# Three-pass float32 products in a gated linear attention block: normalized rows stored split instead of split again in each sweep

## The chip, the cores and the metric

The kernel runs on one core of one Trainium2 chip. The metric is the device time of one execution in microseconds; where several executions are given, the median counts.

## The reference, cut to what matters

One layer of a chunked encoder on 2048 tokens of width 1024. The part that the change touches:

```
h = rmsnorm(x, mix_norm_w)
q, k, v, r, glr = split(h @ gla_w_in)
g = cumsum(log_sigmoid(glr @ w_gate2 + b_gate) / 16)     # in chunks of 64
for each chunk:
    state = state * exp(g_end) + (k * exp(g_end - g)).T @ v
    o = (q / sqrt(128)) @ state
x = x + (rms_normalize(o) * norm_w * silu(r)) @ gla_w_out
x = x + conv_ffn(rmsnorm(x, ffn_norm_w))
out = rmsnorm(x, final_norm_w)
```

## The kernel before, in words

TensorE's float32r operand holds fewer bits than a float32. So every operand is **split** into two float32r tiles: `hi`, a rounded copy made on ScalarE (a CAST), and `lo`, the difference, made on VectorE; the helper `split` (L183 to L186) issues both. A product is then three matmuls (`mm3p`, L173): hi by lo, lo by hi, hi by hi.

The matrix products are cut in seven, after Strassen and Winograd: two token tiles of 128 (a pair `j`, 8 pairs in all) and two column halves make a two by two block matrix, whose seven sums of blocks are called p1 to p7 and run in the order p1, p5, p6, p7, p4, p2, p3. A **row** below is one such sum of normalized input blocks: 128 partitions by 512 float32, 256 KB. There are 56 of them.

The attention part is four sweeps over the 8 pairs, each with other weights (`PS = "RABY"`):

- R makes the rows from x (normalize, transpose, sums), splits each, multiplies it for the gates and for r, and stores the float32 row in DRAM (`h1d`, L368).
- A and B load the 56 rows again, split each again, and multiply for k, q and v of two heads each. Beside the products the scan runs: `scan_tile` (L621) with its small matmuls `pk` and `po`, its transposes `pq` and `px`, and the states `sh`, `sl`. So A and B are the scanning sweeps. `scan_loads` (L604) fetches r from DRAM, and a Silu on ScalarE stands right behind it (L609).
- Y loads scan outputs (`yd`), splits them too and multiplies by w_out.

After that come the two halves of the feed-forward part: U (w_up, with the convolution) and D (w_down). The last 1324 us belong to these.

`prep_row` (L428) fetches a row. In A, B and Y a raw tile (`row_tile`, tag `hr`, `HB = 4` buffers of 2 KB a partition) is loaded for the row itself and the two after it, then `split_row` writes a pair tile (`w_pair`, tag `w`, `WB = 4` buffers of 4 KB). `limit` (L860) says how many rows are prepared before a product: two ahead (`LEAD = 2`). All row loads and stores go through SP's queue, with the loads of r and of E, and the stores of scan outputs. The weights of the next sweep are prepared in the one before: `make_sums` (L264), at pairs 2 and 4, loads weight blocks through ScalarE's queue, adds them on VectorE and stores the sums (`wsd`) through SP's; `plan_w` (L333) then splits the weights around the seam of two sweeps.

The order of instructions on each engine is made ahead of time by a list scheduler that follows the program's priorities and a model of durations; on the chip each engine works through its list in order, DMA issues included.

```
t = w_pair(f"h_{ps_}{j}_{o}")                       # L365
split(t[:, 0, :], t[:, 1, :], src)
if ps_ == "R":
    nc.sync.dma_start(h1d[j, o], src)
```

Of the kernel before, what the change touches and what calls it, by code (L numbers as in the profile page):

```python
# [10 lines left out]
F32 = mybir.dt.float32  # L11
F32R = mybir.dt.float32r
# [4 lines left out]
P = 128  # L17
# [3 lines left out]
def f32(ap):  # L21
    return ap.bitcast(F32)
# [3 lines left out]
def hybrid_kernel(  # L26
# [36 lines left out]
    WB = 4  # L63
    WX = 3
    AB = 6
    HB = 4
    RB = 4
    SB = 8
    YB = 7
    LEAD = 2  # L70
    DLY, KLY, XLY = 5.0, 2.0, 6.5
    NLY, NLE = 5.5, 9.0
    Y0, Y1, U0, U1 = 3.0, 2.8, 14.0, 11.0
# [37 lines left out]
    def scratch(shape, name):  # L111
        return dr.tile(shape, F32, tag=name, name=name)

    x1d = [scratch([P, D], f"x1d_{t}") for t in range(NTT)]
    h1d = {(j, o): scratch([P, 512], f"h1d_{j}_{o}") for j in range(NP) for o in PORD}
    ed = [scratch([P, H * DK], f"ed_{t}") for t in range(NTT)]
    rd = [[scratch([P, 512], f"rd_{t}_{g}") for g in range(2)] for t in range(NTT)]
    yd = {(j, o): scratch([P, 512], f"yd_{j}_{o}") for j in range(NP) for o in PORD}
# [15 lines left out]
    def w_pair(name):  # L134

        return wp.tile([P, 2, 512], F32R, tag="w", name=name, bufs=WB)
# [227 lines left out]
    def split_row(ps_, j, o, src):  # L364
        t = w_pair(f"h_{ps_}{j}_{o}")  # L365
        split(t[:, 0, :], t[:, 1, :], src)
        if ps_ == "R":
            nc.sync.dma_start(h1d[j, o], src)  # L368
        rows[ps_, j, o] = t[:, 0, :], t[:, 1, :]


# [50 lines left out]

    hraw = {}

    def row_tile(name):
        return wp.tile([P, 512], F32, tag="hr", name=name, bufs=HB)

    def prep_row(ps_, j, o):  # L428
        if ps_ == "R":
            need(f"h{j}")  # L430
            if o == "p4":
                diff(j, o, *hsrc.pop(("p4", j)))
            split_row(ps_, j, o, hsrc.pop((j, o)))
        else:
            m = jobs.index((ps_, j, o))
            for n in range(m, min(m + HB - 1, len(jobs))):
                if jobs[n] not in hraw:
                    p_, j_, o_ = jobs[n]
                    hraw[jobs[n]] = row_tile(f"hr_{p_}{j_}_{o_}")
                    nc.sync.dma_start(hraw[jobs[n]], (yd if p_ == "Y" else h1d)[j_, o_])  # L440
            split_row(ps_, j, o, hraw.pop((ps_, j, o)))


# [326 lines left out]
    def prep_h2(jj, raw, pair):  # L770

        s, j = divmod(jj, PAIRS)
        ts = {}
        held = []

        def load(n, c, k):
            if s == 0:
                ts[n] = h2.pop((2 * jj + c, k))
                return
            if n not in ts:  # L780
                ts[n] = raw(f"h2r_{jj}_{n}")
            nc.sync.dma_start(ts[n], h2f[2 * jj + c][:, k, :])

        def store():
            while held:
                o, hl = held.pop(0)
                if s == 0:
                    nc.sync.dma_start(hd[s, o, j], f32(hl))
                else:
                    for i in range(2):  # L790
                        nc.scalar.dma_start(hd[s, o, j][:, i, :], f32(hl[i]))

        def step(o, n, x=None, y=None, then=None):
            store()
            if x is not None:
                nc.vector.tensor_sub(ts[n], ts[x], ts[y])
            if then is not None:
                then()
            hl = pair(f"h2p_{jj}_{o}")
            hi, lo = hl if s else (hl[:, 0, :], hl[:, 1, :])  # L800
            split(hi, lo, ts[n])
            held.append((o, hl))
            later_do(HLY[s], store)

        def first():
            for n, (c, k) in enumerate(((0, 0), (1, 0), (1, 1))):
                load(n, c, k)

        def last():
            store()  # L810
            ready.add(f"h2p{jj}")

        return [
            first, lambda: step("p1", 0), lambda: step("p5", 0, 1, 0), lambda: step("p7", 1, 2, 1),
            lambda: step("p3", 2, then=lambda: load(1, 0, 1)), lambda: step("p6", 0, 2, 0),
            lambda: step("p2", 1), lambda: step("p4", 1, 1, 0), last,
        ]
# [42 lines left out]
    def limit(ps_, j, i):  # L860

        own = (PS.index(ps_) * NP + j + 1) * len(PORD)
        n = own - len(PORD) + i + 1 + LEAD
        if ps_ == "R" and j == 0 and i < len(PORD) - 2:
            return min(n, i + 2)
        if ps_ == "R" and j + 1 < NP:
            return min(n, own + max(0, i - 4))
        return n
# [146 lines left out]
    def phase_u():  # L1015
# [96 lines left out]
        for k, (s, g, o, f) in enumerate(jobs):  # L1112
# [7 lines left out]
            if k == 6:  # L1120
                while delayed:
                    heapq.heappop(delayed)[-1]()
                yp["ctx"].close()
                pools["ctx"] = ExitStack()
                pools["us"] = pools["ctx"].enter_context(tc.tile_pool(name="us", bufs=1, reuse_waits="tile"))
                pools["wx"] = pools["ctx"].enter_context(tc.tile_pool(name="wx", bufs=1, reuse_waits="tile"))
                spread(range(PAIRS, 2 * PAIRS), U0, U1, row_tile,
                       lambda name: tuple(pools["us"].tile([P, 512], F32R, tag="as", name=f"{name}_{i}", bufs=AB) for i in range(2)))
            if s == NS - 1 and g == NQ - 1 and f % 2 == 0:
                d_early(o)  # L1130
# [272 lines left out]
```

## Time and profile before

| what | value |
|---|---|
| median of 3 executions | 2235.53 us (2234.98 to 2243.4) |
| the profiled execution | 2241.04 us |
| its span | 2238.9 us |
| TensorE busy | 2126.9 us (95%) |
| TensorE weight loads busy | 1741.8 us (78%) |
| VectorE busy | 1642.1 us (73%) |
| ScalarE busy | 1107.5 us (49%) |
| moved by DMA | 411.78 MB, mean 184 GB/s |
| mean granted TensorE clock | 0.985 |

Busy times are unions of an engine's instruction intervals; matmuls overlap each other in the records, so the mean length of one (about 0.39 us) is longer than the step from one to the next. The granted clock is a share of full speed (2.4 GHz; the other level is 1.2 GHz). Idle time on an engine that nobody waits for costs nothing.

### The profile page before, as it was taken

The page shows a single profiled execution, that of the slowest core. Times are in us where ns is not written, and L with a number is a line of the kernel's source. Part 1 is how long each engine was busy: PE and PEld are TensorE (multiplying, and loading weights), DVE is VectorE, ACT ScalarE, POOL GpSimd, SP SyncE. Part 2 cuts the span into 40 slices and gives each one's busy share as a digit, 9 for nine tenths or more (in the row PEclk, how much of TensorE's full clock was granted, in tenths as well). Part 3 has the DMA queues.
Part 4 walks back from the last instruction along what each step waited for, and adds up shares of the span by engine and source line. Part 5 has one row for each costly group of instructions (what it writes and reads, how often), then busy time and mean ns, then how long its engine had stood idle before and what let it go on. Part 6 is the DMA issues. An engine that isn't in the chain of part 4 may idle for free.

```text
span 2238.9 us, 29122 instructions
## 1 busy us (share of the span) xinstructions
PE 2126.9 (95%) x9948; PEld 1741.8 (78%) x9948; DVE 1642.1 (73%) x2175; ACT 1107.5 (49%) x2020; POOL 729.1 (33%) x602
## 2 busy tenths in 40 slices
PE   5999999989999899899999999999999999999998
PEld 3788787877887787677787778788888888888886
DVE  7755777788778765388999787797877777557564
ACT  4554655565555576445445444444444543333342
POOL 1000111112111000265566565466655535046100
PEclk9999999999999999999999999999999999999999
DMA  6545684369546799943535428624242468454443
GB/s 209 195 156 185 206 294 126 123 198 325 169 160 196 266 318 335 364 137 123 189 127 163 147 90 282 192 76 136 71 141 71 136 230 321 137 183 151 141 171 116
DMA packets 305077, 411.78 MB, mean 184 GB/s; under 512 B 23694, under 2 KB 160062, under 8 KB 304928
## 3 DMA queue, kind: packets, MB, share of 16 engines
q1 hardware_dynamic: 266156, 346.72, 46.6%
q10 hardware_dynamic: 38772, 63.20, 8.4%
q8 instruction: 78, 1.28, 0.2%
q14 instruction: 71, 0.58, 0.1%
HBM read 266.70 MB, written 143.13 MB: 183 GB/s over the span
## 4 chain that ended last, share of the span: by engine, by line
PE 62%; DVE 14%; DMA 9%; issue 5%; ACT 5%; POOL 3%; SPq 1%; ACTq 0%; DVEq 0%; POOLq 0%
PE pd_p L179 5%; PE pd_p L180 5%; PE pd_p L178 5%; PE ua L178 5%; PE ua L179 5%; PE ua L180 5%; DVE t L1078 4%; PE mp_R L178 2%; PE uc L178 2%; PE uc L180 2%; PE uc L179 2%; PE mp_R L179 2%; PE mp_R L180 2%; DVE uw_p L186 2%; PE mp_A L178 1%
## 5 line engine op out<-in xcount | busy, mean ns | idle before, releaser
L178 PE MATMUL ua<-h_p,uw_p 128*128 128x512 f32 x704 | 280.4, 398 | 24.3 <-ACT c L1060 24.3
L179 PE MATMUL ua<-h_p,uw_p 128*128 128x512 f32 x704 | 278.9, 396 | 0.0
L180 PE MATMUL ua<-h_p,uw_p 128*128 128x512 f32 x704 | 278.5, 396 | 0.0
L1078 DVE SCALAR_TENSOR_TENSOR t<-u,cw,t 128x1024 f32<-128x1024 f32 x176 | 264.2, 1505 | 8.6 <-ACT t L1076 7.5
L179 PE MATMUL pd_p<-dw_p,da 128*128 128x512 f32 x616 | 240.1, 390 | 1.1 <-DVE da L186 1.1
L180 PE MATMUL pd_p<-dw_p,da 128*128 128x512 f32 x616 | 239.9, 389 | 0.0
L178 PE MATMUL pd_p<-dw_p,da 128*128 128x512 f32 x616 | 239.9, 389 | 0.0
L186 DVE TENSOR_TENSOR uw_p<-ur,uw_p 128x512 fp32r<-128x512 f32 x176 | 168.4, 973 | 59.4 <-ACT uw_p L185 52.3
L186 DVE TENSOR_TENSOR da<-da_p,da 128x512 fp32r<-128x512 f32 x154 | 135.6, 933 | 100.5 <-ACT da L185 99.4
L185 ACT CAST da<-da_p 128x512 fp32r<-128x512 f32 x154 | 85.2, 619 | 203.8 <-PE pd_p L180 149.9
L178 PEld LDWEIGHTS ua<-h_p,uw_p 128*128 128x128 f32 x704 | 134.3, 191 | 58.1 <-ACT c L1060 28.6
L185 ACT CAST uw_p<-us 128x512 fp32r<-128x512 f32 x132 | 82.1, 622 | 164.5 <-POOL us L1040 114.1
L186 DVE TENSOR_TENSOR uw_p<-us,uw_p 128x512 fp32r<-128x512 f32 x132 | 122.4, 936 | 53.4 <-ACT uw_p L185 53.0
L180 PEld LDWEIGHTS ua<-h_p,uw_p 128*128 128x128 f32 x704 | 134.2, 191 | 29.9
L179 PEld LDWEIGHTS ua<-h_p,uw_p 128*128 128x128 f32 x704 | 134.4, 191 | 29.4
L178 PE MATMUL uc<-h_p,uw_p 128*128 128x512 f32 x352 | 138.4, 393 | 0.7 <-DMA h_p<-hd_p 0.7
L179 PE MATMUL uc<-h_p,uw_p 128*128 128x512 f32 x352 | 138.1, 392 | 0.0
L180 PE MATMUL uc<-h_p,uw_p 128*128 128x512 f32 x352 | 138.1, 392 | 0.0
L179 PEld LDWEIGHTS pd_p<-dw_p,da 128*128 128x128 f32 x616 | 115.7, 188 | 25.9 <-DVE da L186 1.9
L1076 ACT ACTIVATE t<-u,cw 128x1024 f32<-128x1024 f32 x88 | 109.7, 1247 | 50.9 <-DVE u L1169 43.0
L178 PEld LDWEIGHTS pd_p<-dw_p,da 128*128 128x128 f32 x616 | 115.7, 188 | 24.2
L180 PEld LDWEIGHTS pd_p<-dw_p,da 128*128 128x128 f32 x616 | 115.7, 188 | 23.7
(251 smaller groups left out, 5477.8 us busy)
## 6 DMA issues: line engine op xcount, KB each, us to landing
ur<-in_ffn_w_up_dram SPq DMA_DIRECT2D x168, 256.0 KB, 3.7
da_p<-ad_p SPq DMA_DIRECT2D x154, 256.0 KB, 3.8
h_p<-hd_p SPq DMA_DIRECT2D x56, 512.0 KB, 7.6
ad_p<-as_p SPq DMA_DIRECT2D x88, 256.0 KB, 2.5
ad_p<-t SPq DMA_DIRECT2D x66, 256.0 KB, 3.2
x<-in_x_dram SPq DMA_DIRECT2D x32, 512.0 KB, 4.9
ch<-in_ffn_w_down_dram SPq DMA_DIRECT2D x61, 256.0 KB, 4.0
hr_A_p<-h1d_p SPq DMA_DIRECT2D x56, 256.0 KB, 2.7
```

The lines of the kernel that those rows point to most:

```text
L178: nc.tensor.matmul(ps_ap, ah, bl, start=(first and i == 0), stop=False, **kw)
L179: nc.tensor.matmul(ps_ap, al, bh, start=False, stop=False, **kw)
L180: nc.tensor.matmul(ps_ap, ah, bh, start=False, stop=(last and i == len(pairs) - 1), **kw)
L185: nc.scalar.copy(hi, src)
L186: nc.vector.tensor_sub(lo, src, f32(hi))
L1076: nc.scalar.activation(t, u[:, 2:2 + TS], AF.Identity, scale=cw[:, 2, c:c + 1], bias=cw[:, 3, c:c + 1])
L1078: nc.vector.scalar_tensor_tensor(t, u[:, k:k + TS], cw[:, k, c:c + 1], t, op0=ALU.mult, op1=ALU.add)
```

## The change

Sweep R stores each row as the split pair, hi and lo, 512 KB in place of 256 KB; the store reads the pair tile and so stands behind the split. Sweeps A and B load that pair, straight into a tile that the matmuls read: the 112 CASTs and 112 subtractions of rows in A and B are gone. The `hr` buffers become two of 4 KB a partition in place of four of 2 KB, and A and B use them as pair tiles beside the four `w` tiles, six in all; the loads in A and B are asked for four rows ahead (`ALEAD = 4`), with exceptions in the last pair of B. Sweep Y still splits; there, and where the second half of the feed-forward input is prepared (`prep_h2`), two raw rows share one pair tile.

```diff
--- before.py
+++ after.py
@@ -63,11 +63,11 @@
     WB = 4
     WX = 3
     AB = 6
-    HB = 4
+    HB = 2
     RB = 4
     SB = 8
     YB = 7
-    LEAD = 2
+    LEAD, ALEAD = 2, 4
     DLY, KLY, XLY = 5.0, 2.0, 6.5
     NLY, NLE = 5.5, 9.0
     Y0, Y1, U0, U1 = 3.0, 2.8, 14.0, 11.0
@@ -112,7 +112,7 @@
         return dr.tile(shape, F32, tag=name, name=name)
 
     x1d = [scratch([P, D], f"x1d_{t}") for t in range(NTT)]
-    h1d = {(j, o): scratch([P, 512], f"h1d_{j}_{o}") for j in range(NP) for o in PORD}
+    h1d = {(j, o): scratch([P, 2, 512], f"h1d_{j}_{o}") for j in range(NP) for o in PORD}
     ed = [scratch([P, H * DK], f"ed_{t}") for t in range(NTT)]
     rd = [[scratch([P, 512], f"rd_{t}_{g}") for g in range(2)] for t in range(NTT)]
     yd = {(j, o): scratch([P, 512], f"yd_{j}_{o}") for j in range(NP) for o in PORD}
@@ -365,7 +365,7 @@
         t = w_pair(f"h_{ps_}{j}_{o}")
         split(t[:, 0, :], t[:, 1, :], src)
         if ps_ == "R":
-            nc.sync.dma_start(h1d[j, o], src)
+            nc.sync.dma_start(h1d[j, o], f32(t))
         rows[ps_, j, o] = t[:, 0, :], t[:, 1, :]
 
 
@@ -422,22 +422,29 @@
 
     hraw = {}
 
-    def row_tile(name):
-        return wp.tile([P, 512], F32, tag="hr", name=name, bufs=HB)
+    def row_pair(name, dt=F32):
+        return wp.tile([P, 2, 512], dt, tag="hr", name=name, bufs=HB)
 
     def prep_row(ps_, j, o):
+        m = jobs.index((ps_, j, o))
         if ps_ == "R":
             need(f"h{j}")
             if o == "p4":
                 diff(j, o, *hsrc.pop(("p4", j)))
             split_row(ps_, j, o, hsrc.pop((j, o)))
+        elif ps_ in "AB":
+            n = m - jobs.index(("A", 0, PORD[0]))
+            t = w_pair(f"h_{ps_}{j}_{o}") if n % (WB + HB) < WB else row_pair(f"h_{ps_}{j}_{o}", F32R)
+            nc.sync.dma_start(f32(t), h1d[j, o])
+            rows[ps_, j, o] = t[:, 0, :], t[:, 1, :]
         else:
-            m = jobs.index((ps_, j, o))
-            for n in range(m, min(m + HB - 1, len(jobs))):
+            for n in range(m, min(m + 3, len(jobs))):
                 if jobs[n] not in hraw:
                     p_, j_, o_ = jobs[n]
-                    hraw[jobs[n]] = row_tile(f"hr_{p_}{j_}_{o_}")
-                    nc.sync.dma_start(hraw[jobs[n]], (yd if p_ == "Y" else h1d)[j_, o_])
+                    if (len(jobs) - n) % 2 == 0:
+                        hraw["tile"] = row_pair(f"hr_{p_}{j_}_{o_}")
+                    hraw[jobs[n]] = hraw["tile"][:, (len(jobs) - n) % 2, :]
+                    nc.sync.dma_start(hraw[jobs[n]], yd[j_, o_])
             split_row(ps_, j, o, hraw.pop((ps_, j, o)))
 
 
@@ -778,7 +785,9 @@
                 ts[n] = h2.pop((2 * jj + c, k))
                 return
             if n not in ts:
-                ts[n] = raw(f"h2r_{jj}_{n}")
+                if n != 1:
+                    ts["tile"] = raw(f"h2r_{jj}_{n}")
+                ts[n] = ts["tile"][:, n % 2, :]
             nc.sync.dma_start(ts[n], h2f[2 * jj + c][:, k, :])
 
         def store():
@@ -860,7 +869,9 @@
     def limit(ps_, j, i):
 
         own = (PS.index(ps_) * NP + j + 1) * len(PORD)
-        n = own - len(PORD) + i + 1 + LEAD
+        n = own - len(PORD) + i + 1 + (LEAD if ps_ in "RY" else ALEAD)
+        if ps_ in "AB":
+            return min(n, own) if ps_ == "B" and j + 1 == NP and i < len(PORD) - LEAD else min(n, own + LEAD) if ps_ == "B" and j + 1 == NP else n
         if ps_ == "R" and j == 0 and i < len(PORD) - 2:
             return min(n, i + 2)
         if ps_ == "R" and j + 1 < NP:
@@ -1124,7 +1135,7 @@
                 pools["ctx"] = ExitStack()
                 pools["us"] = pools["ctx"].enter_context(tc.tile_pool(name="us", bufs=1, reuse_waits="tile"))
                 pools["wx"] = pools["ctx"].enter_context(tc.tile_pool(name="wx", bufs=1, reuse_waits="tile"))
-                spread(range(PAIRS, 2 * PAIRS), U0, U1, row_tile,
+                spread(range(PAIRS, 2 * PAIRS), U0, U1, row_pair,
                        lambda name: tuple(pools["us"].tile([P, 512], F32R, tag="as", name=f"{name}_{i}", bufs=AB) for i in range(2)))
             if s == NS - 1 and g == NQ - 1 and f % 2 == 0:
                 d_early(o)
```

The order of the work moves at these places. ScalarE at the first products of sweep A, before (`cp_A` copies a product out of PSUM, `w_A_p` is a weight split, `e` belongs to the gates, `h_A_p` is a row's CAST):

```order
L513 CAST gstk<-pg_2612 32x256
L241 DMA wr_A_2862<-in_gla_w_in_dram 128x2x256
L958 COPY cp_A_2848<-mp_A_2828 128x512
L241 DMA wr_A_2862<-in_gla_w_in_dram 128x2x256
L530 ACT_TABLE_LOAD
L530 ACTIVATE e_0_2870<-pz_0_2868 128x512
L530 ACTIVATE e_1_2874<-pz_1_2872 128x512
L185 CAST w_A_p_2882<-wr_A_2832 128x1024
L958 COPY cp_A_2885<-mp_A_2855 128x512
L185 CAST h_A_p_2889<-hr_A_p_2823 128x512
```

and now:

```order
L520 CAST gstk<-pg_2612 32x256
L241 DMA wr_A_2850<-in_gla_w_in_dram 128x2x256
L185 CAST w_A_p_2870<-wr_A_2823 128x1024
L969 COPY cp_A_2839<-mp_A_2819 128x512
L185 CAST w_A_p_2870<-wr_A_2825 128x1024
L537 ACT_TABLE_LOAD
L537 ACTIVATE e_0_2858<-pz_0_2856 128x512
L537 ACTIVATE e_1_2862<-pz_1_2860 128x512
L969 COPY cp_A_2873<-mp_A_2843 128x512
```

The row's CAST is gone, and a weight CAST stands ahead of the first copy (`wr_A`'s loads are issued by ScalarE itself, `gstk` belongs to the gates). The line numbers of the changed kernel are 5 to 11 higher here. SP's queue in an undisturbed pair of A, before (`hr_A` row loads, `E` and `r` the loads for the scan, `yd` and `b` stores of scan outputs):

```order
L606 DMA E_8_4230<-ed_158 128x256
L440 DMA hr_A_p_4158<-h1d_p_129 128x512
L606 DMA E_9_4263<-ed_159 128x256
L440 DMA hr_A_p_4240<-h1d_p_130 128x512
L440 DMA hr_A_p_4269<-h1d_p_131 128x512
L440 DMA hr_A_p_4331<-h1d_p_132 128x512
L608 DMA r_8_4232<-rd_0_182 128x512
L440 DMA hr_A_p_4363<-h1d_p_133 128x512
```

and now, between the same load of E and the same row:

```order
L613 DMA E_8_4128<-ed_158 128x256
L613 DMA E_9_4158<-ed_159 128x256
L438 DMA h_A_p_4041<-h1d_p_128 128x1024
L438 DMA h_A_p_4059<-h1d_p_129 128x1024
L438 DMA h_A_p_4138<-h1d_p_130 128x1024
L615 DMA r_8_4130<-rd_0_182 128x512
L438 DMA h_A_p_4164<-h1d_p_131 128x1024
L438 DMA h_A_p_4223<-h1d_p_132 128x1024
L715 DMA yd_p_219<-ot_6_4175 128x512
L438 DMA h_A_p_4252<-h1d_p_133 128x1024
```

The second load of E stands ahead of the row loads now, and the load of r two rows earlier among them; the row loads are of twice the size. ScalarE in the second `make_sums` of sweep B, before (`L241` loads of weight blocks into `wm_Y`; `sh` the state's CAST, `og` the squares of the scan's output):

```order
L678 ACTIVATE og_0_5741,ssq_0_5742<-po_0_5728 128x256 x2
L185 CAST sh_1_0_5763<-state_5588 128x512
L241 DMA wm_Y_01_6556<-in_gla_w_out_dram 128x2x512
L185 CAST h_B_p_5827<-hr_B_p_5720 128x512
L707 COPY ot_0_5839<-px_0_5834 128x512
L185 CAST sh_1_1_5776<-state_5588 128x512
L185 CAST vh_3_5794<-o_B_5786 128x512
L609 ACTIVATE r_2_5790<-r_2_5790 128x512
L185 CAST vh_2_5815<-mp_B_5627 128x512
L185 CAST h_B_p_5896<-hr_B_p_5798 128x512
L678 ACTIVATE og_1_5862,ssq_1_5863<-po_1_5849 128x256 x2
```

and now:

```order
L685 ACTIVATE og_0_5534,ssq_0_5535<-po_0_5521 128x256 x2
L185 CAST sh_1_0_5556<-state_5396 128x512
L241 DMA wm_Y_01_6298<-in_gla_w_out_dram 128x2x512
L714 COPY ot_0_5626<-px_0_5621 128x512
L185 CAST vh_3_5587<-o_B_5579 128x512
L185 CAST sh_1_1_5569<-state_5396 128x512
L616 ACTIVATE r_2_5583<-r_2_5583 128x512
L185 CAST vh_2_5605<-mp_B_5429 128x512
L685 ACTIVATE og_1_5649,ssq_1_5650<-po_1_5636 128x256 x2
```

Two row CASTs are gone; the issues of weight loads and the Silu on r stand where they stood, apart from the copy `ot`.

## Rows read from the trace of the kernel before

**Rows 1.** Windows by sweep: us, PE, PEld, DVE, ACT, POOL busy, clock, DMA, GB/s.

```profile
21.00:249.50 228.50, 216.10 (x1243) 175.88 (x1242) 158.32 (x225) 118.51 (x205) 11.41 (x14) 0.99 0.55 184
...
249.50:481.60 232.10, 219.83 (x1135) 183.06 (x1133) 179.07 (x323) 137.32 (x293) 34.26 (x37) 0.98 0.55 178
...
481.60:717.50 235.90, 221.58 (x1154) 183.75 (x1154) 193.15 (x363) 135.88 (x302) 36.22 (x33) 0.99 0.63 211
...
717.50:914.50 197.00, 182.06 (x849) 147.06 (x848) 128.60 (x218) 127.11 (x278) 14.43 (x20) 0.97 0.89 311
```

**Rows 2.** Lines in A, the split: busy us, mean ns, idle before and releaser.

```profile
L186 DVE TENSOR_TENSOR h_A_p<-hr_A_p,h_A_p 128x512 fp32r<-128x512 f32 x54 | 41.9, 776 | 13.5 <-ACT h_A_p L185 13.5
...
L185 ACT CAST h_A_p<-hr_A_p 128x512 fp32r<-128x512 f32 x53 | 32.8, 622 | 5.0 <-PE mp_A L180 4.9
```

**Rows 3.** Lines in B: the subtraction and the Silu on r.

```profile
L186 DVE TENSOR_TENSOR h_B_p<-hr_B_p,h_B_p 128x512 fp32r<-128x512 f32 x56 | 39.2, 701 | 7.4 <-ACT h_B_p L185 6.8
...
L609 ACT ACTIVATE r<-r 128x512 f32<-128x512 f32 x16 | 10.1, 633 | 20.9 <-DMA r<-rd 18.8 <-DVE kd L632 2.0
```

**Rows 4.** Windows inside A and B, with a steady tile pair (374 to 402).

```profile
249.50:272.00 22.50, 19.89 (x81) 15.88 (x79) 17.02 (x20) 18.41 (x27) 4.31 (x2) 0.85 0.53 184
...
290.00:318.00 28.00, 26.00 (x141) 21.61 (x140) 25.89 (x49) 16.58 (x39) 4.54 (x4) 1.00 0.95 312
...
318.00:346.00 28.00, 24.67 (x123) 20.59 (x123) 21.40 (x40) 13.23 (x32) 3.97 (x4) 0.94 0.75 247
...
374.00:402.00 28.00, 27.28 (x146) 22.70 (x145) 20.87 (x41) 15.40 (x37) 4.54 (x4) 1.00 0.38 123
...
481.60:510.00 28.40, 23.54 (x113) 18.71 (x113) 25.97 (x46) 20.05 (x40) 2.66 (x3) 0.94 0.76 254
...
510.00:540.00 30.00, 29.24 (x158) 24.20 (x157) 28.30 (x51) 16.22 (x38) 7.38 (x5) 1.00 0.94 320
...
540.00:570.00 30.00, 26.32 (x134) 22.20 (x133) 22.81 (x45) 15.57 (x37) 4.16 (x5) 0.94 0.80 281
```

**Rows 5.** TensorE timeline: start, length, instruction, idle time before it and what ended that.

```profile
261.64 0.80 PE L178 MATMUL mp_A<-w_A_p,h_A_p 128*128 128x512 f32 x1 [2.61 <-ACT cp_A L958]
...
321.67 0.38 PE L178 MATMUL po<-sl,q 128*128 128x256 f32 x1 [0.92 <-DVE sl L186]
...
339.32 0.60 PE L690 MATMUL px<-ident,og 128*128 128x128 f32 x2 [2.41 <-DVE og L683]
...
395.08 0.44 PE L690 MATMUL px<-ident,og 128*128 128x128 f32 x2 [0.59 <-DVE og L683]
...
477.95 0.39 PE L178 MATMUL po<-sl,q 128*128 128x256 f32 x1 [1.38 <-DVE sl L186]
...
483.56 0.50 PE L179 MATMUL mp_B<-w_B_p,h_B_p 128*128 128x512 f32 x1 [1.30 <-DVE h_B_p L186]
...
495.48 0.50 PE L178 MATMUL mp_B<-w_B_p,h_B_p 128*128 128x512 f32 x1 [2.85 <-ACT cp_B L958]
...
560.37 0.50 PE L178 MATMUL mp_B<-w_B_p,h_B_p 128*128 128x512 f32 x1 [2.33 <-ACT cp_B L958]
```

**Rows 6.** ScalarE timeline, the same columns.

```profile
334.28 0.63 ACT L609 ACTIVATE r<-r 128x512 f32<-128x512 f32 x1 [3.31 <-DMA r<-rd]
...
559.04 0.62 ACT L185 CAST sh<-state 128x512 fp32r<-128x512 f32 x1 [1.97 <-DMA ws_Y_p<-wm_Y]
```

**Rows 7.** Chain of waits, 300 to 340: start and length of a load.

```profile
327.11 7.09 DMA r<-rd
```

**Rows 8.** DMA issues, window 285 to 350: bytes of one, median us to landing.

```profile
ws_B_p<-wm_B SPq DMA_DIRECT2D x8, 512.0 KB, 5.8
...
hr_A_p<-h1d_p SPq DMA_DIRECT2D x15, 256.0 KB, 3.8
```

**Rows 9.** Page, part 6: DMA issues of the whole execution.

```profile
h_p<-hd_p SPq DMA_DIRECT2D x56, 512.0 KB, 7.6
```

**Rows 10.** Waits of SP's queue in sweep R: total us, times, longest.

```profile
SPq L368 <- DVE hb L406: 64.6, 17, 11.4
```

## The prediction

> **What bounds the kernel now.** I read the busy times by sweep first, then the lines of the two removed instructions, then shorter windows, then single stalls of TensorE, and the DMA traffic last.
>
> The windows by sweep stand in the order R, A, B, Y [rows 1]. TensorE is busy 219.83 of 232.1 us in A and 221.58 of 235.9 us in B. So A has 12.3 us and B 14.3 us in which it does nothing, together 26.6 us. However much work the change takes from other engines, that is what it can win, plus what a lower clock after stalls costs. VectorE is busy 179 us in A and 193 us in B, ScalarE 137 and 136 us.
>
> The removed work is large beside this. In A the 54 subtractions on record took 41.9 us and the 53 CASTs 32.8 us [rows 2]; in B the 56 subtractions took 39.2 us [rows 3], and the CASTs are as many and as long as in A. VectorE falls from 77% to about 59% of A and from 82% to about 65% of B. But this counts only where TensorE waits for these two engines.
>
> The windows inside the sweeps show where it does [rows 4]. In an undisturbed pair of tiles (374 to 402) TensorE is busy 27.28 of 28 us at full clock. Its one large gap there, 0.59 us in front of the transposes `px` [rows 5], waits for `og`, the end of a chain from the product `po` over ScalarE, VectorE, GpSimd and VectorE again, in which no row is split. The idle time lies at the seams and around `make_sums`: 249.5 to 272, 290 to 346, 481.6 to 510 and 540 to 570. There the clock is 0.85 and 0.94 too, since TensorE falls from 2.4 to 1.2 GHz for a while after a long stall.
>
> **The change, part by part.**
>
> *Undisturbed pairs: 0.* The gap of 0.59 us recurs some ten times in A and B. An emptier ScalarE and VectorE could shorten it, which bounds the gain at 5.8 us. I take 0, because the chain is latency over four engines and not a queue.
>
> *Waits for VectorE: 3.6 us gained.* Three stalls wait for an operation that stands behind row subtractions in VectorE's list: `sl` 0.92 us and 1.38 us, and the row itself (`h_B`) 1.30 us [rows 5]. Bounds 0 and 3.6; I take them whole, as a subtraction of 0.70 to 0.78 us [rows 2, 3] stood just ahead.
>
> *Waits for ScalarE: 2.6 us gained.* Three stalls wait for a copy `cp` out of PSUM: 2.61, 2.85 and 2.33 us, 7.8 in all [rows 5]. The copy is late for more than row CASTs of 0.62 us: before the stall at 560.37 ScalarE stood still for 1.97 us until the weight sums `ws_Y` had landed [rows 6], and at the seam into A weight CASTs now stand ahead of the first copy. Bounds 0 and 7.8; I take a third, about one or two CASTs per stall.
>
> *Low clock: 2.9 us gained.* Work lost to it is 0.15 x 22.5 = 3.4 us at the first seam, and 0.06 of 28, 28.4 and 30 us in three more windows [rows 4], 5.2 us. Where the stall shrinks by a third I let the loss shrink by a third of 8.6. Bounds 0 and 8.6.
>
> *More traffic in A and B: 3.3 us lost.* A row load grows from 256 to 512 KB. Undisturbed pairs have room: the DMA share there is 0.38 at 123 GB/s. Around `make_sums` they have little. From 290 to 346 two pairs run, 14 rows, so 14 x 256 KB = 3.67 MB are added. The rate at full share is 312 / 0.95 = 328 GB/s [rows 4], so they need 11.2 us, and the engines are idle 0.05 x 28 + 0.25 x 28 = 8.4 us: 2.8 us too much. From 510 to 570, at 4 us a product (28 us for seven), 15 rows add 3.93 MB; at 320 / 0.94 = 340 GB/s they need 11.6 us against 0.06 x 30 + 0.20 x 30 = 7.8 us: 3.8 us too much. The other windows have the room. Of these 6.6 us I count half. The row loads themselves are asked for four rows, some 16 us, ahead of their product and may be late; but `r` and E share SP's queue with them, and the Silu on r blocks ScalarE. In B this Silu already follows 20.9 us of idle time, 18.8 of them ended by the load of r [rows 3].
>
> The Trainium skill judges DMA by bytes and not by busy time ("Perfetto Trace Analysis", Identifying the Most-Contended Engine), against 358 GB/s per core (Engine Utilization). By it the first stretch would fit (345 GB/s with the added bytes) and the second overrun by 1.3 us, so the loss would be 0.7 us in place of 3.3. The rows agree only in part: at 312 GB/s the share already reads 0.95 [rows 4].
>
> The price of a 512 KB row load is bounded by two rows: the store of that size takes 5.8 us around `make_sums`, where a 256 KB row load takes 3.8 [rows 8], and the loads `h_p` of that size take 7.6 us in the later stages [rows 9]. Each is under half of the lead of 16 us. Taken as 6 to 8 us, no row comes late for TensorE; so the row's own wait costs 0.
>
> *Stores in R: 0.* R writes 56 x 256 KB = 14.7 MB more, 45 us of transfer at 328 GB/s, and its DMA engines are idle 0.45 x 228.5 = 103 us [rows 1]. A store now stands behind its split; SP's queue there waits 64.6 us for the raw rows as it is [rows 10], with loads of x behind it. The pair tile is held until the store has landed, 5.8 us by the nearest row, while the four pair tiles give it about 16 us. I take 0, with bounds of -2 (the raw row is free sooner) and +2 us.
>
> *Shared pair tiles in Y: 0.* A raw row's buffer now comes free with its neighbour's, so a load is asked for up to one product, 4 us, later, at a DMA share of 0.89 [rows 1]. Bounds 0 and +4. U and D keep their order.
>
> The sum is -3.6 - 2.6 - 2.9 + 3.3 = -5.8 us. From the profiled execution, 2241.04 us, this gives 2235.2. That execution stands 5.5 us above the median of 2235.53; on the median the forecast is 2235.5 - 5.8 = **2229.7 us**.
>
> **The rivals.**
>
> *VectorE is what holds A and B.* For it: VectorE is the busiest engine after TensorE's matmuls, up to 28.3 of 30 us (510 to 540) and 25.89 of 28 us [rows 4], and `og`, which ends the 2.41 us stall at 339.32 and the 0.59 us ones [rows 5], is its operation. With a quarter of its work gone all gaps would close: 26.6 us, or 2235.5 - 26.6 = 2209 us. Against it: in 510 to 540, where VectorE is fullest, TensorE is idle only 0.8 us. The Trainium skill would have TensorE judged by its weight loads ("Perfetto Trace Analysis", Identifying the Most-Contended Engine). By that VectorE with 193 us stands above weight loads with 184 us in B [rows 1], which speaks for this rival; the windows bear it out where stalls end on VectorE and not in undisturbed pairs. Chance 0.28.
>
> *Slower: r comes late.* The doubled row loads fill the DMA engines around both `make_sums`, r lands later, ScalarE stands in front of its Silu, and behind it wait `og`, the state's CAST and the copies that TensorE needs. One load of r took 7.09 us to land [rows 7], and the Silu waited 3.31 us [rows 6]; TensorE showed 2.41 us of that at 339.32 [rows 5], 0.73 of the wait. So beyond 7.09 - 3.31 = 3.8 us of landing, each us costs 0.73 us. Eight loads of r fall into the two stretches. If each lands 3 us later, this is 8 x 3 x 0.73 = 17.5 us; with 3.6 us from VectorE's waits still won the time is 2235.5 + 17.5 - 3.6 = 2249.4 us. It decides from a landing of r above about 7 us. Against it: r stands two row loads earlier in SP's order. Chance 0.17.
>
> *The change moves nothing.* Every removed instruction was hidden, and the overflow of DMA stays inside the lead: 2235.5 us. For it: 27.28 of 28 us in undisturbed pairs. Chance 0.10.
>
> **How the numbers follow.** The forecast has the remaining 0.45. Its own terms span from all waits, the clock and the steady gaps won and no loss (3.6 + 7.8 + 8.6 + 5.8 = 25.8 us) to nothing won and 6.6 us lost with 6 us in R and Y; its likely part is 2220 to 2240. Half of the first rival lies below 2208 and half of the slower one above 2250, some 0.22 together, so the range is 2208 to 2250. What can be told from no change is 0.5%, 11.2 us. Faster than 2224.3: the first rival nearly whole (0.27) and a fifth of the forecast (0.09), 0.36. Slower than 2246.7: most of the slower rival (0.14) and a little of the forecast, 0.16. Within: 0.48.
>
> **What would show it.** If the steps hold, VectorE's busy time falls by about 81 us and ScalarE's by about 67; the undisturbed pair stays at 28 us with its gap before `px`; the stalls on `sl` and `h_B` are gone, those on `cp` shortened; the row loads take 6 to 8 us around `make_sums` and TensorE never waits for a row; the share there reads near 1. The first rival shows as undisturbed pairs under 27.6 us. The slower rival shows as Silu waits on r of 4 us and more, with TensorE idle behind them. The forecast is wrong if R, Y, U or D change by more than 4 us, or if the windows around `make_sums` grow.

## The result, and the profile after

The changed kernel takes 2249.21 us (median of 8 runs) against 2236.99 us for the kernel before, also of 8: 1.005 times as long, with a 95% interval of 1.0035 to 1.0065. It is slower by some 11 us. The time lies inside the range of the prediction, on the other side of no change. One execution of the run with both placings below took 3145 us at a granted clock of 0.63, and the times here leave it out.

The two profiled executions are only 2.9 us apart in span (2241.8 against 2238.9 us), so the sweeps have to be read one by one. The table takes the first matmul of each sweep from TensorE's timeline, and for the end of Y its last:

```
us                       R      A      B      Y      rest (U and D)
before                   249.6  232.3  235.8  196.8  1324.4
changed                  250.7  236.9  235.7  199.2  1319.3
```

U and D keep their order in both kernels. In the twelve other profiles below they take 1322.8 to 1327.8 us, so 1319.3 is a short draw that hides what was lost ahead of it: 8.0 us by the end of Y. A lost 4.6 us, and B won nothing. R lost 1.1 us and Y 2.4, and neither is told from scatter: three other profiles, of kernels that leave R as it was, begin A at 250.6 to 253.4 us, and Y took 194 to 203 us in all profiles.

The windows by sweep of the kernel after, columns as in [rows 1]:

```profile
21.00:250.70 229.70, 216.61 (x1241) 175.87 (x1241) 155.54 (x221) 117.12 (x202) 11.42 (x14) 0.99 0.67 243
250.70:487.60 236.90, 221.42 (x1137) 183.93 (x1134) 142.19 (x268) 108.29 (x238) 32.15 (x37) 0.97 0.72 247
487.60:723.30 235.70, 219.37 (x1153) 182.57 (x1152) 165.34 (x308) 107.54 (x250) 33.92 (x34) 0.99 0.78 267
723.30:922.50 199.20, 181.92 (x848) 147.24 (x847) 129.81 (x218) 127.31 (x278) 14.52 (x20) 0.96 0.87 304
```

VectorE went from 179 to 142 us in A and from 193 to 165 in B, ScalarE from 137 to 108 and from 136 to 108. That is 65 and 57 us together, where 81 and 67 were expected. TensorE's idle time in A grew all the same, from 12.3 to 15.5 us, and B's from 14.3 to 16.3 us. DMA went from 178 to 247 and from 211 to 267 GB/s. Windows inside the sweeps, to be held against [rows 4]:

```profile
249.50:272.00 22.50, 16.39 (x66) 12.62 (x65) 11.06 (x11) 13.82 (x19) 1.23 (x1) 0.84 0.87 317
296.00:324.00 28.00, 23.64 (x117) 19.15 (x116) 20.93 (x38) 10.12 (x24) 3.75 (x3) 0.94 0.95 334
324.00:352.00 28.00, 25.33 (x136) 20.81 (x135) 16.58 (x37) 11.50 (x30) 3.98 (x4) 1.00 0.86 302
...
404.00:431.60 27.60, 27.02 (x147) 22.61 (x145) 16.07 (x36) 11.79 (x29) 4.10 (x4) 1.00 0.57 191
488.00:516.00 28.00, 21.23 (x101) 17.03 (x101) 20.89 (x35) 16.02 (x33) 2.65 (x3) 0.88 0.70 248
516.00:546.00 30.00, 25.25 (x136) 20.71 (x135) 21.42 (x38) 12.04 (x30) 5.51 (x5) 1.00 0.99 354
546.00:576.00 30.00, 28.28 (x152) 23.42 (x150) 21.53 (x43) 11.26 (x29) 4.04 (x5) 1.00 0.98 343
```

The undisturbed pair got shorter. Of a `make_sums`, the first window got worse and the second better, so the two are taken together: in A TensorE is busy 48.97 of 56 us, where it was 50.67, and in B 53.53 of 60, where it was 55.56. At the seam into A it is busy 16.39 of 22.5 us (it was 19.89), at the seam into B 21.23 of 28 (23.54 of 28.4). So by this trace the two seams have 5.4 us more of idle time and the two `make_sums` 3.7 us, and the rest of A and B has 3.9 us less. TensorE's timeline of the kernel after shows the stalls, columns as in [rows 5]:

```profile
254.69 0.47 PE L178 MATMUL mp_A<-w_A_p,h_A_p 128*128 128x512 f32 x1 [0.96 <-DMA h_A_p<-h1d_p]
261.12 0.66 PE L178 MATMUL mp_A<-w_A_p,h_A_p 128*128 128x512 f32 x1 [2.94 <-ACT cp_A L969]
268.39 0.79 PE L548 MATMUL pd<-ll,later 128*128 128x512 f32 x1 [2.20 <-DVE ll L186]
...
315.11 0.38 PE L178 MATMUL po<-sl,q 128*128 128x256 f32 x1 [4.25 <-DVE sl L186]
339.82 0.74 PE L697 MATMUL px<-ident,og 128*128 128x128 f32 x4 [1.55 <-DVE og L690]
...
403.69 0.44 PE L697 MATMUL px<-ident,og 128*128 128x128 f32 x2 [0.58 <-DVE og L690]
...
431.32 0.44 PE L697 MATMUL px<-ident,og 128*128 128x128 f32 x2 [0.58 <-DVE og L690]
...
493.48 0.44 PE L697 MATMUL px<-ident,og 128*128 128x128 f32 x2 [1.64 <-DVE og L690]
499.63 0.39 PE L661 MATMUL pk<-vl,kz 128*128 128x256 f32 x1 [1.71 <-ACT kz L185]
503.97 0.79 PE L178 MATMUL mp_B<-w_B_p,h_B_p 128*128 128x512 f32 x1 [1.69 <-ACT cp_B L969]
...
542.90 0.38 PE L178 MATMUL po<-sl,q 128*128 128x256 f32 x1 [3.42 <-DVE sl L186]
```

The two large ones, 4.25 and 3.42 us, wait for `sl`, the subtraction of the scan's state. What `sl` waited for is seen on VectorE's timeline: an add of `make_sums` stands in front of it and waits for its weight block.

```profile
313.23 1.23 DVE L275 TENSOR_TENSOR wm_B<-wm_B,wm_B 128x1024 f32<-128x1024 f32 x1 [4.89 <-DMA wm_B<-in_gla_w_in_dram]
314.37 0.69 DVE L186 TENSOR_TENSOR sl<-state,sh 128x512 fp32r<-128x512 f32 x1
```

In B the chain of waits around 540 us (start, length, what) shows the same, link by link:

```profile
533.50 7.39 DMA wm_Y<-in_gla_w_out_dram
...
541.02 1.23 DVE wm_Y L275
542.24 0.61 DVE sl L186
...
542.90 0.38 PE po L178
```

In A two things came together here. The blocks land later; these lines are from 285 to 350 us, before (first the loads of blocks: bytes of one, median us to landing; then the time that VectorE stood idle in front of the adds, and how often):

```profile
wm_B<-in_gla_w_in_dram ACTq DMA_DIRECT2D x8, 256.0 KB, 3.7
...
  DMA wm_B<-in_gla_w_in_dram: 1.2, 1
```

and after:

```profile
wm_B<-in_gla_w_in_dram ACTq DMA_DIRECT2D x8, 256.0 KB, 7.4
...
  DMA wm_B<-in_gla_w_in_dram: 10.5, 4
```

(The 4.7 us that an expectation below names is the median of the whole tile view, which counts stores of the sums with the loads.) In B the blocks land no later than they did; from 495 to 560 us, before:

```profile
wm_Y<-in_gla_w_out_dram ACTq DMA_DIRECT2D x8, 512.0 KB, 6.1
```

and after:

```profile
wm_Y<-in_gla_w_out_dram ACTq DMA_DIRECT2D x8, 512.0 KB, 5.9
```

These medians are of the two to four loads of eight whose landing the trace shows; the one in the chain above took 7.39 us, where the longest before took 6.7. Nor was DMA emptier there: from 516 to 546 us it moved 354 GB/s at a share of 0.99 in both kernels. The row of before:

```profile
516.00:546.00 30.00, 27.97 (x152) 23.16 (x151) 27.01 (x51) 15.23 (x37) 6.97 (x5) 1.00 0.99 354
```

The second thing is that the adds stand earlier in VectorE's list. Without the row subtractions the scheduler takes VectorE to be free and moves the second set of four adds up (`+` an add; the scan's operations by name; here in A):

```
before  vl_3 vl_2 sl_1_1 kd_2 + og_1 kd_3 sl_2_0 + sl_2_1 + +
after   vl_3 + sl_1_1 + vl_2 kd_2 + og_1 +
```

Read so, the row subtractions had been a spacer that filled the time in which a block landed. In B, where the blocks land as before, it is this that is left.

ScalarE waits longer for r too; the lines of the Silu from 249.5 to 720 us, before and after:

```profile
L609 ACT ACTIVATE r<-r 128x512 f32<-128x512 f32 x31 | 19.6, 632 | 28.6 <-DMA r<-rd 26.2 <-DVE kd L632 2.0
```

```profile
L616 ACT ACTIVATE r<-r 128x512 f32<-128x512 f32 x31 | 19.6, 632 | 38.3 <-DMA r<-rd 38.1
```

### The profile page after: what moved, and what is told of

It is laid out like the page before. It is cut to its first block, busy times and chain, and to the rows that moved or that the text cites. A ratio compares the mean times of both kernels' runs of the same rounds, so it can differ in the third digit from the quotient of the medians.

```text
span 2241.8 us, 28799 instructions
## 1 busy us (share of the span) xinstructions
PE 2123.4 (95%) x9948; PEld 1739.3 (78%) x9948; DVE 1584.1 (71%) x2063; ACT 1048.7 (47%) x1908; POOL 720.5 (32%) x602
## 4 chain that ended last, share of the span: by engine, by line
PE 50%; DVE 9%; DMA 7%; issue 4%; POOL 3%; ACT 3%; SPq 1%; ACTq 0%; DVEq 0%; POOLq 0%
PE pd_p L179 6%; PE pd_p L180 6%; PE pd_p L178 6%; PE ua L178 5%; PE ua L179 5%; PE ua L180 5%; DVE t L1089 4%; PE uc L178 2%; PE uc L179 2%; PE uc L180 2%; PE mp_Y L178 2%; DVE uw_p L186 1%; PE mp_Y L179 1%; PE mp_Y L180 1%; PE mp_B L178 1%
## 5 line engine op out<-in xcount | busy, mean ns | idle before, releaser
L178 PE MATMUL pd_p<-dw_p,da 128*128 128x512 f32 x616 | 239.6, 389 | 0.0
```

The lines of the kernel that those rows point to most:

```text
L178: nc.tensor.matmul(ps_ap, ah, bl, start=(first and i == 0), stop=False, **kw)
```

## The experiments

All times stand against the kernel before on the same chip. "Theory 1" is traffic, "theory 2" the order of the adds.

**Traffic taken out.** R stores, and A and B load, the hi parts alone; lo is left out of the products and hi stands in for it.

```diff
-            nc.sync.dma_start(f32(t), h1d[j, o])
-            rows[ps_, j, o] = t[:, 0, :], t[:, 1, :]
+            nc.sync.dma_start(f32(t[:, 0, :]), h1d[j, o][:, 0, :])
+            rows[ps_, j, o] = t[:, 0, :], t[:, 0, :]
```

> The changed kernel with the lo parts neither stored nor loaded (R stores hi alone, A and B load hi alone and use it for lo as well): the row traffic is that of the kernel before, the splits stay away, and the adds of the second set of weight sums still stand ahead of the scan's subtraction sl on VectorE, as in the changed kernel. Theory 1 (doubled traffic makes the weight blocks land late): the loss of some 11 us goes and the 0.3 us per undisturbed pair stay won, so 3 to 8 us faster than the kernel before. Theory 2 (the adds moved ahead of sl, whatever the traffic): still 5 to 9 us slower than before, with TensorE waiting 3 to 4 us for sl in each make_sums.

Measured: 2233.32 us, ratio 0.9986 (0.9973 to 0.9999), some 3 us faster than before and, by the two ratios, 14 us faster than the change. A takes 228.3 us and B 231.5 us, and no stall in the `make_sums` stretches is longer than 1.5 us. In A the adds stand as early as in the changed kernel, the one at 303.6 us right ahead of `sl`, and none of this second set waits for its block; VectorE waits once, 4.4 us, at the first set, and no matmul stands behind that. So in A theory 2 alone falls. In B the order wasn't kept: with shorter loads the scheduler put `sl` (523.3 us) ahead of the add whose block is late (527.5 us, after a wait of 3.3 us). There the run doesn't tell the two theories apart.

With R storing both parts and only the loads halved:

> As the run that stores and loads hi alone, but R stores the whole pair (512 KB); A and B still load hi alone. It prices R's doubled stores by themselves. Theory 1: 1 to 3 us above that run, all of it at the end of R and the seam into A. Theory 2: no difference to it within 1 us.

Measured: 2236.03 us, ratio 0.9991 (0.9977 to 1.0005). The intervals overlap, so R's stores cost no more than a few us; the point values give 1 to 3.

**Traffic put in, order and splits of before.**

```diff
                     nc.sync.dma_start(hraw[jobs[n]], (yd if p_ == "Y" else h1d)[j_, o_])
+                    if p_ in "AB" and "a" in sp:
+                        nc.sync.dma_start(sp["a"].tile([P, 512], F32, tag="dm", ..., bufs=2), h1d[j_, o_])
```

> The kernel before, splits and order kept, with a second load of 256 KB per row in A (from its seventh or so row on) and B into a buffer that nobody reads: the traffic of the change without its order, and without the seam into A. Theory 1: 5 to 10 us slower than before, lost in the two make_sums, where the weight blocks land 6 to 8 us after their issue in place of 4.7. Theory 2: within 2 us of before, since the adds stand behind sl as before.

Measured: 2259.34 us, ratio 1.0094 (1.0078 to 1.0111). The expectation was 5 to 10 us, so this missed. The windows of A and B show that the extra loads didn't lie where the expectation put them: nothing waits for them, the scheduler issued all 103 on record within A (273 GB/s, above the change's 247), and B stayed as it was (212 GB/s).

```profile
250.60:500.80 250.20, 223.76 (x1135) 185.69 (x1133) 176.63 (x323) 137.58 (x293) 31.93 (x37) 0.96 0.83 273
500.80:735.60 234.80, 220.43 (x1153) 182.29 (x1153) 192.92 (x363) 136.06 (x303) 35.59 (x33) 0.99 0.63 212
```

A grew from 232.3 to 250.2 us, B not at all. So traffic costs without the change's order too; here ScalarE's queue paid. In front of the Silu at 346.54 it stood 6.29 us, a wait that the profile puts down to a weight load.

**Order changed, traffic of the change.** Two blocks per pair over pairs 2 to 5, each load released by a one-element write of GpSimd:

```diff
+            for c, src in w_block(ps_, *ij):
+                nc.gpsimd.tensor_copy(r[ij][0:1, 0, c:c + 1], at[0:1, 0:1])
             load_block(nc.scalar, r[ij], ps_, k, ij)
...
+                if o == "p1" and ps_ in "AB" and 2 <= j <= 5:
+                    make_sums(nxt, (j - 2) // 2, j % 2, keep[o])
```

> The changed kernel with the weight blocks for the sums spread over pairs 2 to 5, two blocks per pair: each load waits for a one-element write that GpSimd makes after the first product of its pair, so that the scheduler can't pull all of them together. Traffic is that of the changed kernel plus nothing. Theory 1: the 8 us lost in the two make_sums go; the seam into A (5 us) and R (1.5 us) stay lost and the undisturbed pairs' 0.3 us each stay won, so 2 to 5 us slower than before down to 2 us faster. Theory 2: the same, since the adds no longer stand ahead of a late block; it is told apart by the other runs. If the loss were spread over all of A and B (bandwidth everywhere), it would stay at 8 to 12 us slower.

Measured: 2261.58 us, ratio 1.0097 (1.0077 to 1.0116). This missed, and the miss taught most. Blocks of 256 KB now land in a median of 4.9 us, in place of the change's 7.4, and those of 512 KB in 7.1; but each add stands only as far behind its load as the scheduler takes the load to last, with nothing between them, and VectorE waits longer than ever:

```profile
DVE wm_Y L281 <- DMA wm_Y<-in_gla_w_out_dram: 18.9, 4, 5.5
DVE wm_B L281 <- DMA wm_B<-in_gla_w_in_dram: 13.4, 4, 4.3
```

(total us, times, longest). B went to 251.1 us, with four stalls of 2.4 to 3.2 us on `sl`. So the distance between a load and the in-order engine that meets it counts, and the traffic lengthens what has to be covered.

**Distance given.** Loads released a pair of tiles ahead of the adds, and the adds released later by a scalar of 1.0 (`one`):

```diff
-            fn(dst, x, y)
+            nc.vector.scalar_tensor_tensor(dst, x, one, y, op0=ALU.mult, op1=fn)
...
+                if o == "p1" and ps_ in "AB" and j in (2, 4):
+                    make_sums(nxt, j // 2 - 1, keep[o])
+                if o == "p1" and ps_ in "AB" and j in (1, 3):
+                    load_sums(nxt, j // 2, keep[o])
```

On the changed kernel:

> The changed kernel, all its traffic kept, but with each set of weight blocks loaded a pair of tiles (28 us) ahead of its adds: the loads are released after the first product of pairs 1 and 3, the adds after that of pairs 2 and 4 (through a scalar of 1.0 that GpSimd writes then, so the adds are multiply-adds). Theory 1a (the loss in the make_sums stretches is VectorE and ScalarE standing in their queues for a weight block that lands late): these stalls go, the kernel before's own stalls there too, the seam into A (5 us) and R (1.5 us) stay lost, and the undisturbed pairs' 0.3 us each stay won: 2 to 9 us faster than before. Theory 1b (the DMA engines' rate itself holds A and B, wherever the waits show): the waits move to r or to the rows, and it stays 6 us or more slower than before.

Measured: 2250.53 us, ratio 1.0058 (1.0044 to 1.0071): no gain over the change, though no add waits for a block now. This is what theory 1b expected; the run with r below speaks against it. Against the changed kernel, TensorE's waits for `sl` in A and B fell from 8.7 to 1.6 us, and those for `og` grew from 11.3 to 18.3, with five stalls of 1.9 to 2.75 us. Its timeline shows two of them, and ScalarE's waits what `og` waited for:

```profile
374.07 0.44 PE L708 MATMUL px<-ident,og 128*128 128x128 f32 x2 [1.92 <-DVE og L701]
...
402.69 0.44 PE L708 MATMUL px<-ident,og 128*128 128x128 f32 x2 [2.54 <-DVE og L701]
```

```profile
ACT r L627 <- DMA r<-rd: 41.3, 25, 4.1
```

On the kernel before:

> The kernel before with the same placing of loads and adds of the weight sums as in the run with it on the changed kernel. Theory 1a: its own stalls around make_sums (some 8 us in A and B together with the low clock behind them) go, so 3 to 9 us faster than before, and the difference to that run is the change without the loss at make_sums: seam and R against undisturbed pairs, within 3 us of zero. Theory 1b: within 3 us of before.

Measured: 2232.56 us, ratio 0.9984 (0.9970 to 0.9997): about 4 us faster than before, the fastest complete kernel of this study. A takes 227.3 us, B 233.8. The difference to the changed kernel with the same placing is 0.7%, some 17 us; at most 3 had been expected, so that part missed.

With A's first two rows in SBUF early:

> As the changed kernel with placed loads and adds, but the two pair tiles that R doesn't use take the rows 0 and 1 of A in place of 4 and 5, so that A's first two rows are in SBUF long before the seam. If the row load that TensorE waits for at the seam (0.96 us, and the low clock behind it) is part of the 5 us lost there, 1 to 3 us faster than without; if the seam is lost to the weights' loads alone, no difference within 1 us.

Measured: 2251.48 us, ratio 1.0064 (1.0051 to 1.0077): no difference. The wait for the row (2.05 us in the run without) is gone, and the stall on `cp_A` behind it takes 3.64 us.

**Distance for r as well.** Four buffers for r, and the Silu released after the pair's first product:

```diff
-        r = sp["a"].tile([P, 512], F32, tag="r", name=f"r_{g}_{t}", bufs=2)
+        r = sp["a"].tile([P, 512], F32, tag="r", name=f"r_{g}_{t}", bufs=4)
...
-        nc.scalar.activation(r, r, AF.Silu)
+        nc.scalar.activation(r, r, AF.Silu, scale=one)
```

> The changed kernel with placed loads and adds of the weight sums (as in the run before it), and r besides: four buffers for r in place of two, and the Silu on r released after the first product of its pair, so r has some 28 us to land in place of 3.5. Theory 1a (each doubled stretch costs by the load that an in-order engine stands in front of, first the weight blocks, then r): the five waits for og of 1.9 to 2.75 us in front of px go, so 2236 to 2241 us, within 4 us of before; what is left lost is the seam. Theory 1b (the rate of the DMA engines): the waits move on once more, to the rows or E, and it stays 10 us or more slower than before.

Measured: 2240.89 us, ratio 1.0012 (0.9997 to 1.0027), not told from before and 8 us faster than the change, with all of its traffic. ScalarE's wait for r fell from 38.1 to 0.9 us, VectorE's for blocks from 15.0 us to none. The windows of A and B:

```profile
250.40:482.70 232.30, 217.35 (x1135) 179.75 (x1133) 147.45 (x269) 110.18 (x240) 39.65 (x70) 0.99 0.74 253
482.70:715.30 232.60, 218.56 (x1153) 181.64 (x1153) 161.30 (x307) 108.42 (x248) 39.38 (x61) 0.99 0.79 272
```

More bytes a second than the change (253 and 272 against 247 and 267 GB/s) in less time: the rate of the DMA engines as such doesn't hold A and B.

On the kernel before:

> The kernel before with all of that (weight sums and r). Theory 1a: a little faster than with the weight sums alone, 4 to 8 us faster than before; the difference to the changed kernel with all of it is then the seam (5 us) and R (1.5 us) against 0.3 us per undisturbed pair, within 4 us. Theory 1b: more than 10 us between the two.

Measured: 2247.21 us, ratio 1.0032 (1.0018 to 1.0046). This missed: slower than with the sums alone by some 11 us (by the two ratios), in A (233.4 us) as in B (239.6), with stalls of 1.6 to 1.75 us on `sl` that weren't followed further. So r's part is no plain gain: each of these edits makes the scheduler order everything anew, and what the new order does besides the wait that it was meant for isn't separated. What holds is that with both placings the changed kernel isn't slower than the kernel before with both.

r's part without the sums', on the changed kernel:

> The changed kernel with r's part alone: four buffers for r and the Silu released after the first product of its pair; the weight sums stay as the change left them. With the runs that place the sums alone (no gain over the change) and both (8 to 11 us gained) this makes the four cases. If each wait costs by itself, this one gains the part that r has in the changed kernel, 2 to 5 us, so 2243 to 2247 us. If one late load only takes the other's place, so that a gain needs both, it stays at 2247 to 2252 us.

Measured: 2249.69 us, ratio 1.0042 (1.0025 to 1.0059): no gain. So the four cases on the changed kernel are, as ratios to before, 1.0050 (neither), 1.0058 (sums), 1.0042 (r) and 1.0012 (both). TensorE's waits in A and B, from the profiles:

```
us             for sl   for og   others
neither          8.7     11.3     11.5
sums             1.6     18.3     13.8
r                7.4      8.7     17.2
both             1.9      8.6     17.7
```

With the sums placed, the wait on `sl` is handed on to `og`: there the second wait had hidden behind the first. With r placed alone, `og` and `sl` fall by 3.9 us together and the others grow by 5.7, of which 3.9 are waits for `ll` and for rows at the seam into A. So that only both together gain is shown; that two waits hiding each other are the whole reason is not.

**The seam into A.** Counted in TensorE's matmul columns between 225 and 280 us of the span, taken at full clock, the changed kernel is some 6.8 us of work behind the kernel before, 7.5 with the sums placed, 7.9 with r and 4.2 with both. So part of what both gain lies here. Less row traffic there, lo left out for A's first pair:

> As the changed kernel with all of that, but the seven rows of A's first pair are loaded without their lo parts (hi is used for lo), 1.8 MB less at the seam. If the seam's loss is the DMA traffic there, 2 to 4 us faster than with them; if it is the order of the work at the seam (a weight CAST ahead of the first copy, the gates' ll behind a weight add), no difference within 1 us.

Measured: 2239.69 us, ratio 1.0006 (0.9992 to 1.0020). Less store traffic, lo left out for the rows of the last two pairs:

> The changed kernel with placed sums and r, but for the rows of the last two pairs R stores hi alone, and A and B load hi alone for them: R's last 3.7 MB of doubled stores are gone, the rest stays. If R's stores delay the weight loads of A at the seam, the stall of 1.8 us at the end of R and 1 to 2 us of the seam go, 2 to 4 us faster than with them, with the difference between 225 and 280 us of the span. If they don't, no difference there within 1 us.

Measured: 2240.43 us, ratio 1.0001 (0.9985 to 1.0016). Neither is told from the run with all of the traffic, and by the same count the loss is 3.0 and 6.3 us, with 4.2 in that run. What holds the seam isn't settled. Traffic alone doesn't: with hi alone the loss there is still 3.3 us, and TensorE waits longer than in the changed kernel for `ll`, an operand of the gates that VectorE makes:

```profile
263.31 0.79 PE L548 MATMUL pd<-ll,later 128*128 128x512 f32 x1 [4.86 <-DVE ll L186]
```

In front of that `ll` VectorE had stood 5.42 us for a weight load (5.58 in the changed kernel; 4.95 before, where TensorE has no such stall). The weight loads of A land later there in the changed kernel (256 KB in a median of 4.4 us in place of 3.0, from 225 to 272 us), and they run through four buffers, so delays may add up; this wasn't tried.

## Why the prediction was wrong

**The bound.** The idle 26.6 us of A and B as the most to win, and that only waits on the relieved engines count, held. That VectorE at 193 us in B isn't the bound held too: with 28 us less work there, B didn't get shorter. By the Trainium skill ("Perfetto Trace Analysis", Identifying the Most-Contended Engine) VectorE, above the weight loads in B, was the engine to relieve first. Here the change that relieved it, at the price of more traffic, made the kernel slower.

**Undisturbed pairs, 0.** Nearly right. The gap in front of `px` stays at 0.58 us; from one such gap to the next a pair takes 431.32 - 403.69 = 27.63 us, where it took 27.9. That is 0.3 us per pair, some 2 us over the seven pairs that lie undisturbed in A and B. The first rival's sign was pairs under 27.6 us; they stand at its edge, but the gaps that it would have closed stayed: TensorE's waits for `og` come to 11.3 us in A and B, where they were 11.2.

**Waits for VectorE, 3.6 gained: this step failed first.** I took the subtractions of rows in front of `sl` for a delay that would go. Two of the three stalls did go, the 1.38 us on `sl` and the 1.30 on the row; at that seam others took their place, 1.64 us on `og` and 1.13 and 1.71 on `kz`, an operand of the scan. The third went from 0.92 us to 4.25, and a new one of 3.42 came in B, so that the waits for `sl` rose from 3.9 to 8.7 us in all. The program puts VectorE's free time to use: adds of `make_sums` moved into the place, and these wait for a load. The change's order on VectorE around `make_sums` was the row to read; I had looked there at ScalarE and SP alone.

**More traffic, 3.3 lost: mis-sized.** Places and bytes were right (shares of 0.95 to 0.99 in the first window of each `make_sums`), but I let a transfer cost only what overflows the stretch. A load can land later without that: A's blocks took 7.4 us in place of 3.7 at a share of 0.95 in both kernels. B's took no longer than before. I had named the rows and r as those who might be late, and covered the rows by their lead, rightly: TensorE waited for a row once, 0.96 us. The weight blocks, with a lead of nearly nothing in VectorE's list, I had not costed. That "the other windows have the room" was wrong at the first seam, where TensorE lost 3.5 us of busy time in 22.5, nearly as much as in both `make_sums`; whether by traffic or by order isn't settled. In place of -5.8 us the sum by this profile is: A +4.6, B -0.1, and R +1.1 and Y +2.4 that can't be told from scatter.

The byte rule of the Trainium skill that I weighed against the rows ("Perfetto Trace Analysis", Engine Utilization) would have made the loss smaller still. The row at 354 GB/s and a share of 0.99 lies just under the 358 GB/s that the Trainium skill gives there for a core whose neighbour runs too, and from 526 to 546 us this core, alone, moved 378 GB/s. Neither figure told when a load lands, which is what counted.

**ScalarE, 2.6 gained: about right.** The three stalls on `cp` went from 7.8 to 4.6 us, by 3.2: 2.61 became 2.94, 2.85 became 1.69, and the one of 2.33 in B is gone. **The clock, 2.9 gained: wrong.** Of the four windows at 0.85 and 0.94, the one in B's `make_sums` is back at 1.00, but the seam into A stands at 0.84, one window of A's `make_sums` at 0.94 as before, and the seam into B fell to 0.88, with the other stalls shown there. Over A the mean fell from 0.98 to 0.97, over B it stayed at 0.99.

**The slower rival** gave 2249.4 us, and the time is 2249.2. That the number fits is luck: its sum takes 17.5 us from eight late loads of r and gives 3.6 back on VectorE, and neither came: TensorE's waits for `og`, behind r, stayed where they were. Its sign, Silu waits on r of 4 us and more with TensorE idle behind them, didn't show either (the longest was 3.9 us). Its place (both `make_sums`, though not the seams) and form (a load that lands late in front of an in-order engine) were right. Its load was the wrong one: r cost TensorE more only when the weight blocks were out of the way. I gave it 0.17, where its row, a landing of 7.09 us, was already in the trace before.

**R's stores and Y's shared tiles, 0.** Within the bounds: 1.1 us in R and 2.4 in Y, both inside the scatter.

## What to carry to other kernels

Work that an engine is relieved of may have been the distance between a load and its use: read, in the new order, what moves into its place, and whether that waits for a DMA. Trading compute for traffic cost here through loads with a short lead in front of an in-order engine, and not through the rate of the DMA engines, which carried more in less time once those loads had distance. List such loads with their leads, and give them distance before adding bytes. A wait that is mended can hand its time on to the next one, so that mending it alone shows no gain. And where a scheduler orders everything anew, read the whole new order: r's edit, put on top of the sums', gained on one of these kernels and lost on the other.

## What was not expected of the hardware

Landing times stretched with DMA far from full in the mean: at shares of 0.72 and 0.78 in A and B, where it was 0.55 and 0.63, the median landing of r rose from 2.7 to 3.9 us (of the 10 loads before and 15 after whose landing the trace shows). And with enough distance the same core carried 253 and 272 GB/s through A and B in 232.3 and 232.6 us, no longer than the kernel before with 178 and 211.
